# Stored low halves of projection weights, another start, and a multiply with paired operands, in a decoder-block kernel

## The chip, the cores and the metric

The kernel runs on one core of a Trainium2 chip. The metric is the device time of one execution in microseconds (us).

## The reference

One decoder block on 1024 tokens of width 1024, in float32. The conditioning vector gives six modulation vectors; two sub-layers follow, each with a norm, a shift and scale, and a gated residual.

```python
mod = silu(c) @ w_ada + b_ada
sh1, sc1, g1, sh2, sc2, g2 = split(mod, 6)
h = rms_norm(x, norm1_g) * (1 + sc1) + sh1
b_gate, c_gate, hc, q, k, v = split(h @ w_in, splits)
mixed = [norm(short_conv(b_gate, c_gate, hc)), norm(window_attention(q, k, v, rel_bias, sinks))]
x = x + g1 * (mixed @ w_out)
h2 = rms_norm(x, norm2_g) * (1 + sc2) + sh2
x = x + g2 * peer_ffn(h2, wq, keys, u_tab, v_tab)
```

`peer_ffn` scores each token against two sets of 128 keys for each of 8 heads, adds the best 16 of each set in pairs, keeps the best 16 sums, and uses those experts out of 16384 (one row of `u_tab`, one of `v_tab` each). The attention has a window of 128 and a bias per head that depends on the distance only, through 32 buckets.

## The kernel before

The tokens go through `front()` in three groups of 384, 384 and 256. A group takes 18 projections by `w_in` (keys, queries, values, and three per chunk of the convolution), the attention, 8 projections by `w_out`, and 16 by `wq`, each of the last followed by scores and a search for the 16 best. After the third group `dense()` multiplies 640 tokens with the whole expert tables and gathers single rows for the other 384.

**A projection** (`proj`, lines 260 to 274) is 42 times a group the same step: two half tiles of 128x512 (256 KB) are loaded by SP (L265). ACT casts each to `wH`, a rounded form in which TensorE (PE) multiplies fast (L268); POOL subtracts to get the rest `wL` (L269); then per half 12 matmuls, high by high, high by low and low by high (L272). `wraw`, `wH` and `wL` have three buffers each. The three groups use the same weights, so each half tile is loaded, cast and subtracted three times, 84 subtracts a group.

**Beside the projections of groups 2 and 3** run pieces of the group before, handed out by credit at each projection (`bg`, L227): `select` (the best 16 sums, then one-hot products that pick indices) and `spread`, which builds for each token a one-hot matrix `oi`, scaled, and another `oj`, multiplies them on PE (L714), copies the product to `stage` (ACT, L715), and stores `stage` in pieces of 2 MB (L717, SP). A block of 128 tokens needs 128 `oi`, dealt to the engines by the pattern `HOT = "APVV"`: 32 on ACT (L703, L704), 32 on POOL and 64 on VectorE (called DVE; both L706), and 32 `oj` on DVE (L711). The first five of the eight blocks go through `spread`; all eight go through `select`, six of them beside groups 2 and 3. In `select`, L660 compares a 128x2048 bf16 tile with ranks and L662 multiplies it by the indices `idf`, broadcast along the innermost axis; both run twice a block.

**The start** (`ada_start`, L182): parts 1 and 0 of the modulation, eight tiles of 512 KB each, arrive in turn. Part 1 is summed on DVE (L190, L192), and part 0 by PE with 128 matmuls of one column (L194). Meanwhile the statistics of the first norm are taken, and POOL scales `x` by them (L1038). Then `bias_table` (L206) makes the attention bias: each head one matmul of 32 buckets (L217), to which DVE adds a mask (L219), one by one between the first projections.

The order of instructions on each engine comes from a list scheduler over the whole program, not from the order of the lines. SP issues its DMAs strictly in that order, and one that waits holds up all that stand behind it.

Of the kernel before, what the change touches and what calls it, by code (L numbers as in the profile page):

```python
# [10 lines left out]
F32 = mybir.dt.float32  # L11
# [10 lines left out]
P = 128  # L22
# [52 lines left out]
def hymba_peer_kernel(ctx: ExitStack, tc: tile.TileContext, a, out: bass.AP):  # L75
# [39 lines left out]
    biasd = dram.tile([P, NH, 384], F32, name="biasd")  # L115

# [65 lines left out]
    def ada_start(ap, ring, acc):  # L182

        mps0 = pm.tile([P, 8], F32, name="pm")
        for c in range(NC):
            w1, w0 = ring[2 * c % len(ring)], ring[(2 * c + 1) % len(ring)]
            nc.sync.dma_start(w1, a["w_ada"][1, :, c, :])
            nc.sync.dma_start(w0, a["w_ada"][0, :, c, :])
            if c == 0:
                V.tensor_scalar(acc, w1, cond[:, c:c + 1], None, op0=ALU.mult)  # L190
            else:
                V.scalar_tensor_tensor(acc, w1, cond[:, c:c + 1], acc, op0=ALU.mult, op1=ALU.add)  # L192
# [3 lines left out]
            yield  # L196
        mps = pm.tile([P, 8], F32, name="pm")
        for m in range(NC):
            PE.matmul(mps[:, m:m + 1], acc[:, P * m:P * (m + 1)], ones[:, 0:1], start=True, stop=True)
        b0 = COLS["b"][0]  # L200
        V.tensor_add(mod[:, 8:16], mps, cols[:, b0 + 8:b0 + 16])
        V.scalar_tensor_tensor(gs[:, 0:8], mod[:, 8:16], 1.0, colr("g1"), op0=ALU.add, op1=ALU.mult)
        V.tensor_add(mod[:, 0:8], mps0, cols[:, b0:b0 + 8])
        done.extend((1, 0))

    def bias_table(ap):  # L206
        relb = ap.tile([32, NH], F32, name="relb", bufs=1)
        nc.sync.dma_start(relb, a["rel_bias"])
        bkt = ap.tile([32, 384], F32, name="bkt", bufs=1)
        nc.sync.dma_start(bkt, a["bucket"])  # L210
        bmask = ap.tile([P, 384], F32, name="bmask", bufs=1)
        nc.sync.dma_start(bmask, a["bmask"])
        rb = ap.tile([32, NH, P], F32, name="rb", tag="acc", bufs=1)
        V.tensor_copy(rb, relb.unsqueeze(2).to_broadcast([32, NH, P]))
        for h in range(NH):
            bp = pm.tile([P, 384], F32, name="pm")
            PE.matmul(bp, rb[:, h, :], bkt, start=True, stop=True)  # L217
            bt = ap.tile([P, 384], F32, name="bt", bufs=1)
            V.tensor_add(bt, bp, bmask)  # L219
            nc.sync.dma_start(biasd[:, h, :], bt)  # L220
            yield
# [3 lines left out]
    tasks, rest, table = [], [], []  # L225
# [61 lines left out]
    def norm_mod(chunk, gsc, shc, H, L, T, scaled=False, r=None):  # L287
        if not scaled and r is None:
            r = norm_stats(chunk, T)
        for c in range(NC):  # L290
# [41 lines left out]
    def front(t0, T, hs, nxt):  # L332
# [9 lines left out]
        A.copy(kc, proj(a["w_in"][4], hH, hL, T))  # L342
        qT = [tmp("y", bufs=4)[:, 0:T] for c in range(4)]
        for c in range(4):
            A.copy(qT[c], proj(a["w_in"][c], hH, hL, T))
        vT = tmp("q")
        A.copy(vT[:, 0:T], proj(a["w_in"][5], hH, hL, T))

        def conv():
            ys = []  # L350
            for cc in range(4):
                cs = tmp("q")[:, 0:T]
                A.copy(cs, proj(a["w_in"][6 + 3 * cc], hH, hL, T))
# [3 lines left out]
                V.tensor_tensor(u[:, 2:T + 2], cs, proj(a["w_in"][7 + 3 * cc], hH, hL, T), op=ALU.mult)  # L357
# [6 lines left out]
                V.tensor_tensor(y, y, proj(a["w_in"][8 + 3 * cc], hH, hL, T), op=ALU.mult)  # L364
# [34 lines left out]
        drain(table[0])  # L399
# [90 lines left out]
        for c in range(NC):  # L490
            pt = proj(a["w_out"][c], mH, mL, T)
# [101 lines left out]
    def select(va, iu):  # L593
        idf = sel.tile([P, 2 * PH, 16], BF16, name="idf")
        A.copy(idf, iu)
        va4 = va.rearrange("p (h s) k -> p h s k", s=2)
        id4 = idf.rearrange("p (h s) k -> p h s k", s=2)
        cand = sel.tile([P, PH, NCAND], F32, name="cand")
# [58 lines left out]
        for s, src in ((0, aab), (1, stb)):  # L657
# [4 lines left out]
            V.tensor_tensor(hot1, hot1, id4[:, :, s, :].unsqueeze(3).to_broadcast([P, PH, 16, 16]), op=ALU.mult)  # L662
# [357 lines left out]
    with tc.tile_pool(name="ada", bufs=2, side="right") as ap:  # L1020
# [5 lines left out]
        first = ada_start(ap, slots[0:3] + wide, slots[3])  # L1026
# [7 lines left out]
        for _ in range(3):  # L1034
            next(first)
# [94 lines left out]
```

## Time and profile before

| | |
|---|---|
| median of 3 runs | 2853.47 us (2850.66 to 2859.0) |
| profiled execution, its own time | 2857.49 us |
| span of the profiled execution | 2855.7 us |
| granted TensorE clock, mean | 0.979 |
| PE matmul busy | 2700.5 us, 95% |
| DVE busy | 2373.4 us, 83% |
| ACT busy | 1093.9 us, 38% |
| POOL busy | 1721.7 us, 60% |
| DMA moved | 764.31 MB, 268 GB/s over the span |

The first 1022 us are the three groups, the rest is the dense part. Shares over the whole span are mostly those of the dense part, so for a change in the groups each stage has to be read by itself: group 1 ends at 335 us, the `w_in` projections of group 2 at 530, its `w_out` and `wq` projections at 724, those of group 3 at 876 and 1022. A busy PE is not a PE at its peak: matmuls are pipelined, and each is shown until its modelled end.

### The profile page before, as it was taken

The page shows a single profiled execution, that of the slowest core. Times are in us where ns is not written, and L with a number is a line of the kernel's source. Part 1 is how long each engine was busy: PE and PEld are TensorE (multiplying, and loading weights), DVE is VectorE, ACT ScalarE, POOL GpSimd, SP SyncE. Part 2 cuts the span into 40 slices and gives each one's busy share as a digit, 9 for nine tenths or more (in the row PEclk, how much of TensorE's full clock was granted, in tenths as well). Part 3 has the DMA queues.
Part 4 walks back from the last instruction along what each step waited for, and adds up shares of the span by engine and source line. Part 5 has one row for each costly group of instructions (what it writes and reads, how often), then busy time and mean ns, then how long its engine had stood idle before and what let it go on. Part 6 is the DMA issues. An engine that isn't in the chain of part 4 may idle for free.

```text
span 2855.7 us, 45148 instructions
## 1 busy us (share of the span) xinstructions
PE 2700.5 (95%) x15679; PEld 2445.9 (86%) x15679; DVE 2373.4 (83%) x4845; ACT 1093.9 (38%) x2193; POOL 1721.7 (60%) x1491
## 2 busy tenths in 40 slices
PE   8899988999787889999999999999999999999998
PEld 6788978789786778889989989999989889988987
DVE  3665898877899697888988888888889888888887
ACT  2455468775586643222322222232222222222221
POOL 3444475656667744666666666666666666666661
PEclk7999999999999989999999999999999999999999
DMA  7647423464344677999999999999999999999995
GB/s 243 217 155 232 121 103 115 158 216 156 97 151 137 234 227 229 342 337 343 326 322 346 340 344 335 349 325 332 347 334 324 325 339 346 333 336 345 324 327 193
DMA packets 345157, 764.31 MB, mean 268 GB/s; under 512 B 31296, under 2 KB 130016, under 8 KB 341984
## 3 DMA queue, kind: packets, MB, share of 16 engines
q0 software_dynamic: 112320, 408.99, 39.6%
q1 hardware_dynamic: 231168, 349.81, 37.4%
q8 instruction: 123, 2.02, 0.3%
q10 hardware_dynamic: 1440, 2.62, 0.2%
q14 instruction: 106, 0.87, 0.1%
HBM read 702.06 MB, written 59.24 MB: 267 GB/s over the span
## 4 chain that ended last, share of the span: by engine, by line
PE 44%; DMA 8%; DVE 6%; issue 5%; POOL 2%; ACT 1%; SPq 0%; DVEq 0%; POOLq 0%; ACTq 0%
PE pv L873 22%; PE pa L816 21%; DMA vraw<-in_v 4%; DMA uraw<-in_uT 2%; DVE pq L768 2%; DVE vdL L860 1%; POOL rows L741 1%; ACT vdH L859 1%; DVE rows L760 1%; DMA wraw<-in_wq 1%; DMA rows<-in_v,eidx 1%; POOL uL L800 1%; DVE dacc L892 0%; DVE gw L835 0%; PE pj L272 0%
## 5 line engine op out<-in xcount | busy, mean ns | idle before, releaser
L816 PE MATMUL pa<-h,uH 128*128 128x320 f32 x4096 | 772.9, 311 | 15.2 <-ACT uH L799 6.2
L816 PEld LDWEIGHTS pa<-h,uH 128*128 128x128 f32 x4096 | 648.8, 189 | 23.1 <-ACT uH L799 7.2
L873 PE MATMUL pv<-vdH,wdH 128*128 128x512 f32 x1275 | 500.0, 392 | 18.0 <-DVE dacc L892 16.4
L269 POOL TENSOR_TENSOR wL<-wraw,wH 128x512 fp32r<-128x512 f32 x252 | 351.5, 1402 | 272.7 <-ACT wH L268 249.4
L873 PE MATMUL pv<-vdL,wdH 128*128 128x512 f32 x1275 | 497.8, 390 | 0.1
L873 PE MATMUL pv<-vdH,wdL 128*128 128x512 f32 x1275 | 496.8, 390 | 0.0
L816 PE MATMUL pa<-h,uL 128*128 128x320 f32 x2048 | 469.2, 310 | 2.3 <-POOL uL L800 2.3
L800 POOL TENSOR_TENSOR uL<-uraw,uH 128x512 fp32r<-128x512 f32 x256 | 342.4, 1338 | 163.3 <-ACT uH L799 142.7
L741 POOL DMA_INDIRECT rows<-in_u,eidx x257 | 260.8, 1015 | 157.1 <-DVE aw L760 83.2
L741 POOL DMA_INDIRECT rows<-in_v,eidx x254 | 253.7, 999 | 164.6 <-DVE pq L768 117.1
L816 PEld LDWEIGHTS pa<-h,uL 128*128 128x128 f32 x2048 | 344.6, 189 | 3.3 <-POOL uL L800 3.3
L768 DVE SCALAR_TENSOR_TENSOR pq<-rows,aw,pq 128x1024 f32<-128x1024 f32 x253 | 324.5, 1282 | 3.3 <-DMA rows<-in_v,eidx 0.8
L892 DVE TENSOR_TENSOR dacc<-dacc,pv 128x512 f32<-128x512 f32 x310 | 211.9, 684 | 134.0 <-PE pv L873 111.4
L859 ACT CAST vdH<-vraw 128x512 fp32r<-128x512 f32 x255 | 153.5, 619 | 439.0 <-DMA vraw<-in_v 366.4
L799 ACT CAST uH<-uraw 128x512 fp32r<-128x512 f32 x256 | 158.3, 619 | 418.9 <-DMA uraw<-in_uT 340.5
L760 DVE CUSTOM_DVE_ANT_0 rows<-rows,pq 128x1024 f32<-128x1024 f32 x257 | 307.5, 1212 | 12.5 <-DMA rows<-in_u,eidx 10.9
L873 PEld LDWEIGHTS pv<-vdH,wdH 128*128 128x128 f32 x1275 | 239.6, 188 | 74.9 <-DVE dacc L892 24.7
L873 PEld LDWEIGHTS pv<-vdH,wdL 128*128 128x128 f32 x1275 | 239.8, 188 | 50.9
L873 PEld LDWEIGHTS pv<-vdL,wdH 128*128 128x128 f32 x1275 | 239.8, 188 | 47.3 <-DVE vdL L860 0.5
L706 POOL TENSOR_SCALAR oi<-iota,tr 128x128 f32<-128x128 f32 x160 | 198.5, 1243 | 96.2 <-PE gps L714 88.1
L860 DVE TENSOR_TENSOR vdL<-vraw,vdH 128x512 fp32r<-128x512 f32 x255 | 192.1, 770 | 71.7 <-ACT vdH L859 66.7
L842 ACT CAST wdH<-gw 128x640 fp32r<-128x640 f32 x128 | 93.0, 728 | 377.0 <-DVE gw L835 342.4
(257 smaller groups left out, 5085.7 us busy)
## 6 DMA issues: line engine op xcount, KB each, us to landing
uraw<-in_uT SPq DMA_DIRECT2D x256, 256.0 KB
vraw<-in_v SPq DMA_DIRECT2D x255, 256.0 KB
gd<-stage SPq DMA_DIRECT2D x20, 2048.0 KB
gt<-gd SPq DMA_DIRECT2D x160, 256.0 KB
wraw<-in_w_in SPq DMA_DIRECT2D x108, 256.0 KB
wraw<-in_wq SPq DMA_DIRECT2D x96, 256.0 KB
wt<-in_w_ada SPq DMA_DIRECT2D x40, 512.0 KB
wraw<-in_w_out SPq DMA_DIRECT2D x48, 256.0 KB
```

What stands on the lines that cost most here:

```text
L269: G.tensor_tensor(wL, w, wH.bitcast(F32), op=ALU.subtract)
L706: (G if who == "P" else V).tensor_scalar(oi, iota, tr[:, 0, t:t + 1], tr[:, 2, t:t + 1], op0=ALU.is_equal, op1=ALU.mult)
L741: G.indirect_dma_start(out=r, out_offset=None, in_=table, in_offset=bass.IndirectOffsetOnAxis(ap=eidx[:, ti, k:k + 1], axis=0))
L760: V.tensor_tensor_reduce(out=r, in0=r, in1=h2, op0=ALU.mult, op1=ALU.add, scale=1.0, scalar=0.0, accum_out=aw[:, k:k + 1])
L768: V.scalar_tensor_tensor(acc, r, aw[:, k:k + 1], acc, op0=ALU.mult, op1=ALU.add)
L799: A.copy(uH, raw)
L800: G.tensor_tensor(uL, raw, uH.bitcast(F32), op=ALU.subtract)
L816: PE.matmul(AT[j][:, s, 0:n], l[:, c, :], h2[r][4 * h + c][:, s * n:s * n + n], start=(h == 0 and c == 0 and k == 0), stop=(h == 1 and c = ...
L859: A.copy(vH, raw)
L860: V.tensor_tensor(vL, raw, vH.bitcast(F32), op=ALU.subtract)
L873: PE.matmul(pt, l[:, P * tt:P * tt + P], r, start=(m == 0), stop=(m == 3 * J - 1))
L892: V.tensor_tensor(dst, dst, pt, op=ALU.add)
```

## The change

It has three parts.

1. **Stored low parts.** `proj` takes a name and an index. In the first group it keeps POOL's subtract and stores each `wL` to DRAM (`save`, one tile later); in groups 2 and 3 it loads `wL` by SP instead of subtracting. `wL` gets four buffers.
2. **The start.** Both parts are summed on DVE, part 1 first, then part 0; 8 matmuls with ones add up each. The bias table's 8 matmuls move to the beginning: the mask is a 33rd bucket with weight one, ACT copies the results out, and SP stores all 8 behind the last tile of part 0. `x` is no longer scaled by POOL; the first norm uses the way of the others, except that every second low part is made by ACT and POOL.
3. **Pairs in `select`.** ACT writes each index twice side by side (two copies a block instead of one), so that the second operand of the multiply (L662) ends in two adjacent bf16 values instead of a broadcast.

```diff
+    def save(keep):
+        while len(unsaved) > keep:
+            key, wL = unsaved.pop(0)
+            lows[key] = dram.tile([P, 4, P], F32, name="low_{}{}{}".format(*key))
+            nc.sync.dma_start(lows[key], wL.bitcast(F32))
+
-    def proj(wsrc, sH, sL, T):
+    def proj(name, m, sH, sL, T):
+        wsrc = a[name][m]
...
-            wL = wp.tile([P, 4, P], F32R, name="wL")
+            wL = wp.tile([P, 4, P], F32R, name="wL", bufs=4)
             A.copy(wH, w)
-            G.tensor_tensor(wL, w, wH.bitcast(F32), op=ALU.subtract)
+            if (name, m, h) in lows:
+                nc.sync.dma_start(wL.bitcast(F32), lows[name, m, h])
+            else:
+                G.tensor_tensor(wL, w, wH.bitcast(F32), op=ALU.subtract)
+                save(1)
+                unsaved.append(((name, m, h), wL))
```

```diff
-    def ada_start(ap, ring, acc):
...
-            for m in range(NC):
-                PE.matmul(mps0[:, m:m + 1], w0[:, P * m:P * (m + 1)], cond[:, c:c + 1],
-                          start=(c == 0 and m == 0), stop=(c == NC - 1), skip_group_check=True)
...
+    def ada_start(ring, accs):
...
+        for i in (1, 0):
+            for c in range(NC):
+                wt = ring[n % len(ring)]
+                nc.sync.dma_start(wt, a["w_ada"][i, :, c, :])
+                if c == 0:
+                    V.tensor_scalar(accs[i], wt, cond[:, c:c + 1], None, op0=ALU.mult)
+                else:
+                    V.scalar_tensor_tensor(accs[i], wt, cond[:, c:c + 1], accs[i], op0=ALU.mult, op1=ALU.add)
...
+        def fill():
+            for h in range(NH):
+                bp = pm.tile([P, 384], F32, name="pm")
+                PE.matmul(bp, rb[:, h, :], bkt, start=True, stop=True)
+                A.copy(bts[h], bp)
...
-        for c in range(NC):
-            G.tensor_tensor(x0c(c), x0c(c), r0[:, 0:T0], op=ALU.mult)
...
+            if shared and c % 2:
+                A.activation(t, t, AF.Identity, bias=shc(c))
+                G.tensor_tensor(lo, t, h.bitcast(F32), op=ALU.subtract)
```

```diff
-        idf = sel.tile([P, 2 * PH, 16], BF16, name="idf")
-        A.copy(idf, iu)
+        idf = sel.tile([P, 2, PH * 16, 2], BF16, name="idf")
+        iu4 = iu.rearrange("p (h s) a -> p h s a", s=2)
+        for s in range(2):
+            A.copy(idf[:, s].rearrange("p (h a) y -> p h a y", h=PH),
+                   iu4[:, :, s, :].unsqueeze(3).to_broadcast([P, PH, 16, 2]))
...
-            V.tensor_tensor(hot1, hot1, id4[:, :, s, :].unsqueeze(3).to_broadcast([P, PH, 16, 16]), op=ALU.mult)
+            hk = hot1.rearrange("p h a (k y) -> p (h a) k y", y=2)
+            V.tensor_tensor(hk, hk, idf[:, s].unsqueeze(2).to_broadcast([P, PH * 16, 8, 2]), op=ALU.mult)
```

The order on three engines, before and then changed. First POOL, beside the `w_out` and `wq` projections of group 2 before (`mc` is the convolution's low part):

```order
L706 TENSOR_SCALAR oi<-iota,tr 128x128 x2
L269 TENSOR_TENSOR wL<-wraw,wH 128x512
L706 TENSOR_SCALAR oi<-iota,tr 128x128
L269 TENSOR_TENSOR wL<-wraw,wH 128x512 x2
L706 TENSOR_SCALAR oi<-iota,tr 128x128 x5
L373 TENSOR_TENSOR mc_3988<-y,mc_3987 128x384 x4
L706 TENSOR_SCALAR oi<-iota,tr 128x128 x3
L269 TENSOR_TENSOR wL<-wraw,wH 128x512 x4
```

and POOL in the change, from the attention of group 2 into group 3 (L732 is the old L706, L397 the old L373):

```order
L732 TENSOR_SCALAR oi<-iota,tr 128x128 x44
L397 TENSOR_TENSOR mc_4104<-y,mc_4103 128x384 x3
L732 TENSOR_SCALAR oi<-iota,tr 128x128
L397 TENSOR_TENSOR mc_4104<-y,mc_4103 128x384
L732 TENSOR_SCALAR oi<-iota,tr 128x128 x43
L405 TENSOR_TENSOR kL<-k,kH 128x256
```

All subtracts for `wL` are gone from POOL in groups 2 and 3; what it has left there is `oi` and a few low parts of activations.

Next SP in the `w_in` projections of group 2, around the first store of `stage`, before:

```order
L265 DMA wraw_4176<-in_w_in 128x512
L265 DMA wraw_4194<-in_w_in 128x512
L265 DMA wraw_4355<-in_w_in 128x512
L265 DMA wraw_4373<-in_w_in 128x512
L717 DMA gd_87<-stage_3405 128x4096
L265 DMA wraw_4494<-in_w_in 128x512
```

and changed:

```order
L286 DMA wraw_4292<-in_w_in 128x512
L291 DMA wL_4200<-low_w_in71_791 128x512
L286 DMA wraw_4310<-in_w_in 128x512
L291 DMA wL_4295<-low_w_in80_882 128x512
L286 DMA wraw_4471<-in_w_in 128x512
L291 DMA wL_4313<-low_w_in81_902 128x512
L286 DMA wraw_4489<-in_w_in 128x512
L743 DMA gd_87<-stage_3521 128x4096
L291 DMA wL_4474<-low_w_in90_952 128x512
L286 DMA wraw_4611<-in_w_in 128x512
```

SP issues twice as many loads, and the load of a low part stands one or two places behind the load of the next `wraw`; the store of `stage` stands between them as before.

Last DVE at the start (`wt`, `wringa` and `wringb` are tiles of `w_ada` and the sums), before:

```order
L284 RECIPROCAL rstd<-rstd 128x384
L192 SCALAR_TENSOR_TENSOR wt<-wringb_145,cond,wt 128x1024
L192 SCALAR_TENSOR_TENSOR wt<-wt,cond 128x1024
L192 SCALAR_TENSOR_TENSOR wt<-wringa_142,cond,wt 128x1024
L192 SCALAR_TENSOR_TENSOR wt<-wringb_144,cond,wt 128x1024
L201 TENSOR_TENSOR mod<-pm,cols 128x8
L202 SCALAR_TENSOR_TENSOR gs<-mod,cols 128x8
L203 TENSOR_TENSOR mod<-pm,cols 128x8
```

and changed:

```order
L222 TENSOR_SCALAR wt<-wringa_142,cond 128x1024
L224 SCALAR_TENSOR_TENSOR wt<-wringa_143,cond,wt 128x1024
L230 TENSOR_TENSOR mod<-pm,cols 128x8
L224 SCALAR_TENSOR_TENSOR wt<-wringb_144,cond,wt 128x1024
L231 SCALAR_TENSOR_TENSOR gs<-mod,cols 128x8
L320 SCALAR_TENSOR_TENSOR t<-x_140,gs,rstd 128x384
L224 SCALAR_TENSOR_TENSOR wt<-wringb_145,cond,wt 128x1024
L320 SCALAR_TENSOR_TENSOR t<-x_140,gs,rstd 128x384
L224 SCALAR_TENSOR_TENSOR wt<-wt,cond 128x1024 x2
L233 TENSOR_TENSOR mod<-pm,cols 128x8
```

The second half of `mod` now waits for eight more sums on DVE instead of PE's matmuls, and two of the first norm's products stand between them.

## Rows read from the trace of the kernel before

**Rows 1.** Busy time by stage: us, each engine's busy time (instructions), PEclk, DMA share, GB/s.

```profile
0.00:335.00 335.00, 304.71 (x1618) 270.01 (x1619) 200.19 (x564) 146.66 (x315) 148.08 (x111) 0.91 0.61 198
335.00:530.00 195.00, 172.15 (x1106) 154.59 (x1104) 184.00 (x633) 138.43 (x342) 123.41 (x95) 0.97 0.37 126
530.00:724.00 194.00, 181.72 (x1117) 166.93 (x1118) 146.89 (x509) 122.34 (x273) 118.32 (x95) 0.98 0.50 168
724.00:876.00 152.00, 123.42 (x902) 110.02 (x901) 138.01 (x502) 103.81 (x255) 104.58 (x76) 0.96 0.38 129
876.00:1022.00 146.00, 125.61 (x952) 116.60 (x951) 113.70 (x389) 89.99 (x204) 106.25 (x87) 0.98 0.56 187
```

**Rows 2.** PE's instructions in time, group 2: start us, us, engine, line, tile.

```profile
...
404.77 0.34 PE L272 MATMUL pj<-hH,wH 128*128 128x384 f32 x1
...
407.37 0.34 PE L272 MATMUL pj<-hH,wH 128*128 128x384 f32 x1
408.33 1.60 PE L714 MATMUL gps<-oj,oi 128*128 128x128 f32 x12 [0.62 <-ACT stage L715]
```

**Rows 3.** Groups of PE instructions, 335 to 530 us: xcount | busy us, mean ns.

```profile
L714 PE MATMUL gps<-oj,oi 128*128 128x128 f32 x400 | 55.9, 283 | 9.2 <-DVE oi L706 3.7 <-ACT stage L715 2.5 <-DVE oj L711 1.3
```

**Rows 4.** Groups of DVE instructions by form, 335 to 1022 us, same columns.

```profile
L706 DVE TENSOR_SCALAR oi<-iota,tr 128x128 f32<-128x128 f32 x320 | 123.5, 424 | 22.9 <-PE gps L714 21.5
L711 DVE TENSOR_TENSOR oj<-iota,tr 128x512 f32<-128x512 f32 x160 | 122.4, 783 | 4.7 <-PE gps L714 2.8 <-ACT tr L690 1.4 <-issue 0.2
...
L660 DVE TENSOR_TENSOR hot<-stb,rank 128x2048 bf16<-128x2048 bf16 x6 | 7.3, 1214 | 0.0
```

**Rows 5.** Durations of tile oi in ns, min/median/max, 335 to 1022 us.

```profile
L706 DVE TENSOR_SCALAR oi<-iota,tr x320: 240/340/1379, 378.5 to 968.8; 128x128 f32<-128x128 f32 x160
```

**Rows 6.** The same of tile oj.

```profile
L711 DVE TENSOR_TENSOR oj<-iota,tr x160: 637/683/1793, 377.3 to 967.0; 128x512 f32<-128x512 f32 x160
```

**Rows 7.** POOL in time, 384 to 391 us, columns as in rows 2.

```profile
384.37 2.78 POOL L706 TENSOR_SCALAR oi<-iota,tr 128x128 f32<-128x128 f32 x2
387.12 1.27 POOL L269 TENSOR_TENSOR wL<-wraw,wH 128x512 fp32r<-128x512 f32 x1
```

**Rows 8.** DVE in time, the same stretch.

```profile
385.20 1.28 DVE L711 TENSOR_TENSOR oj<-iota,tr 128x512 f32<-128x512 f32 x2
...
387.27 1.67 DVE L711 TENSOR_TENSOR oj<-iota,tr 128x512 f32<-128x512 f32 x1
```

**Rows 9.** Busy time of L662 by stage: us, DVE busy (instructions), PEclk, DMA.

```profile
335.00:530.00 195.00, 11.49 (x5) 0.97 0.37 126
530.00:724.00 194.00, 2.29 (x1) 0.98 0.50 168
724.00:876.00 152.00, 10.73 (x4) 0.96 0.38 129
876.00:1022.00 146.00, 5.74 (x2) 0.98 0.56 187
```

**Rows 10.** Who waited for whom, 335 to 1022 us: total us, times, longest.

```profile
PE pj L272 <- POOL wL L269: 17.2, 15, 5.5
PE pj L272 <- ACT wH L268: 7.9, 5, 4.1
```

**Rows 11.** The waits of SP's queue, the same stretch.

```profile
SPq L717 <- ACT stage L715: 59.9, 9, 19.3
SPq L717 <- ACT oi L703: 36.0, 6, 14.7
```

**Rows 12.** DVE in time at the start.

```profile
15.30 1.28 DVE L192 SCALAR_TENSOR_TENSOR wt<-wt,cond 128x1024 f32<-128x1024 f32 x1 [6.67 <-DMA wt<-in_w_ada]
```

**Rows 13.** PE in time at the start.

```profile
41.14 3.55 PE L194 MATMUL pm<-cond,wt 128*128 128x1 f32 x16
...
53.18 0.69 PE L272 MATMUL pj<-hH,wH 128*128 128x384 f32 x1
...
59.08 0.91 PE L217 MATMUL pm<-bkt,rb 32*128 32x384 f32 x2
```

More of the change, by code (lines that the diff above doesn't have):

```diff
@@ L214, in bias_table @@
[L214 to L221, printed above, removed]
+        V.memset(rb, 1.0)
+        V.tensor_copy(rb[0:32], relb.unsqueeze(2).to_broadcast([32, NH, P]))
+        bts = [tmp("q") for _ in range(4)] + [tmp("y", bufs=4) for _ in range(4)]
@@ new lines, in fill, with store, total @@
+        def fill():
[3 more added lines that the diff above has]
+                A.copy(bts[h], bp)
+        def store():
+            for h in range(NH):
+                nc.sync.dma_start(biasd[:, h, :], bts[h])
+        return fill, store
+    def ada_start(ring, accs):
+        b0 = COLS["b"][0]
+        mps = [pm.tile([P, 8], F32, name="pm") for _ in range(2)]
+        def total(i):
+            for m in range(NC):
+                PE.matmul(mps[i][:, m:m + 1], accs[i][:, P * m:P * (m + 1)], ones[:, 0:1],
+                          start=True, stop=True)
+        n = 0
+        for i in (1, 0):
[6 more added lines that the diff above has]
+                    V.scalar_tensor_tensor(accs[i], wt, cond[:, c:c + 1], accs[i], op0=ALU.mult, op1=ALU.add)
+                if c == NC - 1 and i:
+                    total(1)
+                n += 1
+                yield n
+        total(0)
+        V.tensor_add(mod[:, 8:16], mps[1], cols[:, b0 + 8:b0 + 16])
+        V.scalar_tensor_tensor(gs[:, 0:8], mod[:, 8:16], 1.0, colr("g1"), op0=ALU.add, op1=ALU.mult)
+        yield n + 1
+        V.tensor_add(mod[:, 0:8], mps[0], cols[:, b0:b0 + 8])
+        done.extend((1, 0))
@@ L352, in conv @@
                 cs = tmp("q")[:, 0:T]
-                A.copy(cs, proj(a["w_in"][6 + 3 * cc], hH, hL, T))
+                A.copy(cs, proj("w_in", 6 + 3 * cc, hH, hL, T))
                 yield
@@ L1025, in hymba_peer_kernel @@
         wide = [t.rearrange("p c t -> p (c t)")[:, 0:D] for t in bigt(ba, "wringa", F32) + bigt(bb, "wringb", F32)]
-        first = ada_start(ap, slots[0:3] + wide, slots[3])
-        next(first)
-        for h in range(2):
-            nc.sync.dma_start(x0[h][:, :, 0:T0], a["xT"][:, 4 * h:4 * h + 4, 0:T0])
+        fill, store = bias_table(ap)
+        first = ada_start(slots[0:2] + wide, slots[2:4])
         def x0c(c):
             return ch(x0, c)[:, 0:T0]
-        for _ in range(3):
-            next(first)
-        r0 = norm_stats(x0c, T0)
-        for c in range(NC):
-            G.tensor_tensor(x0c(c), x0c(c), r0[:, 0:T0], op=ALU.mult)
-        for _ in first:
-            pass
-        hs = norm1(*GROUPS[0], x0c)
-        table.append(add(bias_table(ap), 1.0))
+        for n in first:
+            if n == 3:
+                for h in range(2):
+                    nc.sync.dma_start(x0[h][:, :, 0:T0], a["xT"][:, 4 * h:4 * h + 4, 0:T0])
+                fill()
+                pt0 = pj.tile([P, TM], F32, name="pj")
+                for c in range(NC):
+                    sq = tmp("sq")
+                    A.activation(sq[:, 0:T0], x0c(c), AF.Square)
+                    PE.matmul(pt0[:, 0:T0], onesd, sq[:, 0:T0], start=(c == 0), stop=(c == NC - 1))
+                r0 = tmp("rstd", bufs=2)
+                A.activation(r0[:, 0:T0], pt0[:, 0:T0], AF.Sqrt, bias=epsc)
+            if n == 2 * NC + 1:
+                V.reciprocal(r0[:, 0:T0], r0[:, 0:T0])
+        store()
+        hs = norm1(*GROUPS[0], x0c, r0)
         rest.append(add(ada((2, 4, 3, 5), ap, slots), ADA_RATE, ADA0))
         hs, prev = front(*GROUPS[0], hs, nxts[0])
+        save(0)
         for t in rest:
```

60 lines of the change are left out of this document (17 added, 43 removed).

## The prediction, made before the changed kernel was run

> **What bounds the kernel now.** I read first the busy time by stage, because the page's shares are those of the dense part. In the `w_in` stages of groups 2 and 3 (335 to 530 and 724 to 876 us) DVE is busy for 184.00 and 138.01 us, together 93% of 347 us; in the two stages of `w_out` and `wq` PE leads with 181.72 of 194 and 125.61 of 146 us, and DVE has 77% [rows 1]. PE's figures flatter it: in order of time the projections' matmuls start 0.173 us apart (2.60 us for 15 steps) but are shown 0.34 us long, and those of `spread` start 0.12 us apart (12 in 1.60 us, the last 0.28) [rows 2]. So 36 half tiles of 12 matmuls are 75 us and 400 matmuls of `spread` [rows 3] 48 us, 123 of the 195 us; attention adds some. PE could go faster there. For `w_out` and `wq` of group 2 the same count, 48 half tiles, is 100 us, plus `spread`, scores, transposes and norms, and I see little air. So: **DVE sets the pace of the `w_in` stages, PE and DVE share the others.**
>
> Next I ask what DVE's time consists of. By form, `oi` takes 424 ns and `oj` 783 ns on average [rows 4], yet their medians are 340 and 683 ns, their least 240 and 637 [rows 5, 6]. In order of time one sees why: two `oj` beside POOL's `oi` took 0.64 us each, and the next, beside POOL's subtract `wL`, took 1.67 us [rows 7, 8]. A subtract on POOL, which reads two tensors, makes a DVE instruction of two tensors wait.
>
> **The sum.** The change takes 84 subtracts from POOL in each of groups 2 and 3, 168 at 1.27 us [rows 7].
>
> *Relief of DVE.* Mean less median: (424-340) x 320 = 26.9 us for `oi`, (783-683) x 160 = 16.0 us for `oj` [rows 4 to 6]. L662 took 30.25 us for 12, 2.8 us over its free price of 2.29 us [rows 9]. That is 45.7 us in groups with 276 of DVE's 583 us; the others have fewer instructions with two tensors, and at a third of that rate give 15 more: 60 us, an estimate. Half of it I put into the `w_in` stages, which are half of the time. There L662 adds the pairs: a multiply that runs as L660 does, on the same 128x2048 bf16, would take 1.21 instead of 2.29 us [rows 4, 9]; 9 of the 12 lie there, 9 x 1.08 = 9.7 us. Of 39.7 us I let 93% come through, DVE's busy share: **-37**. The ends are -9, if the stretches stay, and -50, if two thirds lie here and all comes through. In the `w_out` and `wq` stages the other 30 us and 3 x 1.08 us fall on a DVE that is 77% busy beside a PE that is fuller; a third, **-11**, between 0 and -33.
>
> Which POOL instructions stretch DVE decides this term, and the rows above part them by one example. The Trainium skill, "SBUF — State Buffer", section "Who interferes with whom", says that a DVE instruction with two SBUF inputs contends with any GpSimd instruction that reads SBUF. By that rule POOL's `oi` would hold up `oj` as the subtract does, which the 0.64 us in rows 8 speak against; by it the term would be about half (the first rival), by the row it is the whole.
>
> *PE's own waits.* PE waited 17.2 us for `wL` from POOL [rows 10]. The part in DVE-bound time is covered; a third: **-5**, between 0 and -17.
>
> *The start.* Now PE's matmuls for part 0 end at 41.14 + 3.55 = 44.7 us [rows 13]. Changed, DVE has 16 sums of 1.28 us [rows 12], 20.5 us, and about 4 us for the reciprocal and two products that stand among them (an estimate from sizes like these), from 15.3 us on [rows 12]: 39.8 us. Half of `mod` is then still to be added up by 8 matmuls; 16 records of such one-column matmuls (two each) take 3.55 us [rows 13], so it is ready at 43.3 us, some 1 to 2 us sooner. The first projection's matmul starts at 53.18 us, and the table's matmuls come in pieces of 0.91 us between projections, as at 59.08 us [rows 13]. Four of these go, 3.6 us and as much again as they wait for, at most; taken 4. One more for the four that stood ahead of it. Together **-7**, between +3 (if DVE is stretched by 4 us more) and -10.
>
> *Stores.* 84 stores of 256 KB, 22 MB in the 335 us of group 1, are 66 GB/s on top of 198, with the DMA engines at 0.61 [rows 1]. They wait behind POOL, which they don't hold up; but in SP's order they can delay a `wraw`. Nearest row: PE's waits for `wH`, which comes from a load, 7.9 us in two groups [rows 10]. **+2**, from 0 to 8.
>
> *Loads.* In groups 2 and 3 SP loads 168 x 256 KB more, which takes the stages from between 126 and 187 GB/s [rows 1] to between 183 and 261 (22 MB over 389 and over 298 us). By rows 2 a half tile lasts at least 2.1 us on PE and 5.4 us on average in the stage of 195 us; with four buffers a load has three of them to land in. As many `wraw` loads cost PE 7.9 us [rows 10]; the new ones have less lead: **+5**, from 0 to 16 (twice that row).
>
> *At nothing:* the second copy of the indices lies on ACT, busy 71% at most in these stages [rows 1], ahead of a multiply that comes two steps later; `cand` shares `hot1`'s buffer, and DVE itself reads the one out before it writes the other. DVE's next wait, once it is faster, is for PE to free `oi` buffers, 21.5 us today [rows 4].
>
> Sum: -37 -11 -5 -7 +2 +5 = -53. From the profiled execution's 2857.5 us that is 2804.5; the median of the runs stands 4.0 us below that execution, so **2800 us**. A measurement of this kernel can tell about 0.3% from no change, 8.6 us.
>
> **The rivals.**
>
> *Half of the relief.* POOL's `oi`, now back to back, stretch DVE in the subtract's place. Subtracts are 168 x 1.27 = 213 us [rows 7] of POOL's 453 us in these stages [rows 1], so half of the 60 us would stay: -23 -6 -5 -7 +7 = -34, 2819 us. For: the part left to POOL reads SBUF too. Against: rows 7 and 8. Chance 0.13.
>
> *All of it.* Each us of DVE and each wait counts once: 60 + 13 + 17 + 7 less 2 of cost = -95, 2758 us. For: 93% busy; against: PE's fullness between 530 and 724 us. Chance 0.12.
>
> *Pairs don't pack.* If the multiply keeps 2.29 us, 9.7 x 0.93 + 3.2 / 3 = 10 us are lost: 2810 us. For: its second operand is still a broadcast over eight; against: L660's operands have a broadcast as well. Chance 0.08.
>
> *Slower.* SP issues in order, and its stores of `stage` waited 59.9 us for the copy to `stage` and 36.0 us behind ACT's `oi`, at most 19.3 us at a time [rows 11]. Today `wraw`, `wH` and `wL` with three buffers each give about six half tiles of lead; a loaded `wL` has three that PE still holds. Wherever a store waits longer than those last, 6 us at full pace and 16 us at the average, PE stops. If all 96 us reach PE: 2857.5 - 53 + 96 - 4 = 2896 us. For: 15 waits of 6.4 us on average; against: at the stages' pace most are shorter than the cover. Chance 0.07.
>
> *No change.* `spread` is a ring of PE, ACT and DVE through few buffers; if that ring sets the pace, relief turns into waits for PE: about 2853 us. Against: those waits are only 21.5 us today. Chance 0.06.
>
> **Numbers.** The forecast has 0.54; alone it spans 2775 to 2830 us. The range, 2756 to 2838 us, reaches over the two cases of relief and, at the top, over half relief with loads at their dear end; it leaves out no change, slower, and tails. Faster by over 0.3%: 0.54 + 0.13 + 0.12 + 0.08 = 0.87; within: 0.06; slower: 0.07.
>
> **What would show it.** Right: `oi` and `oj` on DVE with means near 340 and 683 ns, L662's successor at 1.2 us, the `w_in` stages of groups 2 and 3 shorter by about 37 us together and the others by 10, the first projection ending some 7 us sooner, group 1 otherwise as long as now. Wrong: means of `oj` still near 730 ns beside POOL's `oi`; PE waiting for loads of `wL` by more than 16 us; SP's waits at stores followed by gaps on PE; or a DVE that is idle for PE in the time it gained.

## The result, and the profile after

The changed kernel takes **2822.22 us** (median of 4 runs, 2820.88 to 2823.97) against 2856.23 us (4 runs) before: a ratio of 0.9883, 95% interval 0.9862 to 0.9903, 34 us faster. The forecast was 2800 us. The profiled execution has a span of 2820.3 us, 35.4 less than before.

Where the 35.4 us came from shows a table that is worked out from the starts and ends of the projections' matmuls in the two traces, in us: `start` is the first of them; `in1` the `w_in` stage of group 1 and `rest1` what follows up to the end of the group; `in23` the `w_in` stages of groups 2 and 3, `rest23` all else of these groups; `dense` from the last projection to the end.

```
             start    in1  rest1   in23 rest23   dense    span
before        53.2  140.0  142.3  342.5  344.0  1833.6  2855.7
after         54.0  137.7  150.2  294.5  340.2  1843.6  2820.3
```

The `w_in` stages give 48.0 us and `rest23` 3.8; the start costs 0.8, group 1 after it 5.6 and the dense part 10.0. Busy time by stage of the changed kernel, with columns as in [rows 1]:

```profile
0.00:342.00 342.00, 286.41 (x1510) 247.22 (x1511) 206.52 (x569) 151.96 (x328) 132.57 (x101) 0.93 0.77 259
342.00:512.00 170.00, 163.01 (x1097) 149.71 (x1096) 155.25 (x627) 136.90 (x342) 75.79 (x57) 0.99 0.56 193
512.00:707.00 195.00, 182.42 (x1128) 169.43 (x1127) 136.02 (x513) 122.05 (x276) 59.66 (x48) 0.96 0.69 239
707.00:832.00 125.00, 112.77 (x886) 104.69 (x885) 114.84 (x476) 101.17 (x252) 46.48 (x40) 0.99 0.68 234
832.00:977.00 145.00, 129.12 (x969) 122.45 (x967) 100.61 (x412) 92.98 (x212) 45.93 (x40) 0.94 0.77 269
```

In the four stages of groups 2 and 3 DVE is busy for 506.7 us where it was 582.6: 76 us less. Taken from the first to the last projection matmul of the two `w_in` stages, DVE's busy time fell from 317.6 to 269.6 us, by as much as these stages got shorter. Taken in the same way beside `w_out` and `wq`, it fell from 237.1 to 212.8 us, yet these stages did not get shorter (314.7 us before, 315.7 now); the 3.8 us of `rest23` lie in the pieces between the stages. The granted TensorE clock fell there: 0.96 and 0.94 above, 0.98 twice in [rows 1]. It stood at 1.2 GHz, the lower of its two levels, for 28.8 us of these stages, before for 6.8 us. The longest stretch, 618 to 632 us, began while PE waited for ACT's copy to `stage`:

```profile
620.47 2.93 PE L740 MATMUL gps<-oj,oi 128*128 128x128 f32 x12 [5.04 <-ACT stage L741]
...
618.00:632.00 14.00, 9.86 (x41) 9.30 (x42) 11.77 (x55) 6.91 (x16) 3.29 (x4) 0.51 0.65 225
```

22 us more at half the clock cost at most 11 us, an estimate. DMA carries 193 to 269 GB/s there instead of 126 to 187 and is nowhere full on average. The groups of DVE's instructions by form, 342 to 977 us (xcount | busy us, mean ns | idle before):

```profile
L737 DVE TENSOR_TENSOR oj<-iota,tr 128x512 f32<-128x512 f32 x160 | 107.6, 688 | 5.5 <-PE gps L740 3.6 <-ACT tr L716 0.3
L732 DVE TENSOR_SCALAR oi<-iota,tr 128x128 f32<-128x128 f32 x320 | 104.0, 361 | 39.4 <-PE gps L740 37.2 <-ACT h2H L321 0.4 <-ACT tr L716 0.2
...
L688 DVE TENSOR_TENSOR hot<-hot,idf 128x2048 bf16<-128x2048 bf16 x12 | 14.6, 1218 | 0.1
```

`oj` went from 783 to 688 ns and `oi` from 424 to 361 [rows 4], almost to their medians of before, and the multiply (L662, now L688) from 2.5 us to 1.22 us [rows 9]. The waits of PE, DVE and POOL in the same stretch:

```profile
POOL oi L732 <- PE gps L740: 161.5, 71, 10.4
...
DVE oi L732 <- PE gps L740: 37.2, 39, 7.1
...
PE pj L298 <- DMA wL<-low_wq: 3.4, 2, 2.7
```

POOL and DVE now wait longer for PE to free buffers for `oi` (DVE 37.2 us, 21.5 before [rows 4]). The increase lies beside `w_out` and `wq`: in the `w_in` stages DVE's waits of this kind, for `oi` and `oj` together, are 9.0 us and were 10.2. PE waits 3.4 us for loaded `wL` of `wq` and 1.4 us for those of `w_in`, where it waited 17.2 us for POOL [rows 10]. And SP's queue:

```profile
SPq L291 <- PE pj L298: 192.9, 110, 11.7
...
SPq L743 <- ACT stage L741: 17.8, 12, 6.6
...
SPq L743 <- ACT oi L729: 13.0, 3, 10.5
```

Its waits at the stores of `stage` for ACT's copy and `oi` fell from 95.9 us [rows 11] to 30.8; what it waits for most now is PE, which frees the buffers of `wL`.

At the start DVE and PE read as follows, in order of time:

```profile
18.41 1.28 DVE L224 SCALAR_TENSOR_TENSOR wt<-wringa,cond,wt 128x1024 f32<-128x1024 f32 x1 [4.13 <-DMA wringa<-in_w_ada]
...
26.56 2.55 DVE L1071 RECIPROCAL rstd<-rstd 128x384 f32<-128x384 f32 x1 [4.22 <-ACT rstd L1069]
...
35.74 0.17 DVE L230 TENSOR_TENSOR mod<-pm,cols 128x8 f32<-128x8 f32 x1 [2.47 <-PE pm L213]
...
48.39 0.17 DVE L233 TENSOR_TENSOR mod<-pm,cols 128x8 f32<-128x8 f32 x1 [3.67 <-PE pm L213]
...
54.00 0.69 PE L298 MATMUL pj<-hH,wH 128*128 128x384 f32 x1 [5.65 <-ACT wH L289]
```

DVE stood idle for 4.13 us at a tile, 4.22 us ahead of the reciprocal, which waited for the statistics (their matmuls stood behind the bias table's eight on PE), 2.47 us ahead of the first add to `mod`, and had the second at 48.39 us instead of 44.7 [rows 13].

### The profile page after: what moved, and what is told of

It is laid out like the page before. It is cut to its first block, busy times and chain, and to the rows that moved or that the text cites. A ratio compares the mean times of both kernels' runs of the same rounds, so it can differ in the third digit from the quotient of the medians.

```text
span 2820.3 us, 45052 instructions
## 1 busy us (share of the span) xinstructions
PE 2672.6 (95%) x15567; PEld 2428.3 (86%) x15567; DVE 2301.1 (82%) x4846; ACT 1097.0 (39%) x2213; POOL 1477.2 (52%) x1315
## 4 chain that ended last, share of the span: by engine, by line
PE 52%; DVE 7%; DMA 7%; issue 4%; ACT 2%; POOL 1%; SPq 0%; DVEq 0%; POOLq 0%; ACTq 0%
PE pv L899 25%; PE pa L842 22%; DMA vraw<-in_v 4%; PE pj L298 2%; PE gps L740 1%; DVE vdL L886 1%; DVE rows L786 1%; DVE pq L794 1%; DMA uraw<-in_uT 1%; DMA wraw<-in_wq 1%; POOL uL L826 1%; DVE dacc L918 1%; DVE gw L861 1%; DVE more L786 1%; DVE wdL L869 0%
## 5 line engine op out<-in xcount | busy, mean ns | idle before, releaser
L732 POOL TENSOR_SCALAR oi<-iota,tr 128x128 f32<-128x128 f32 x160 | 203.1, 1273 | 350.4 <-PE gps L740 161.5
L289 ACT CAST wH<-wraw 128x512 fp32r<-128x512 f32 x252 | 154.6, 618 | 165.9 <-PE pj L298 77.3
```

The lines of the kernel that those rows point to most:

```text
L732: (G if who == "P" else V).tensor_scalar(oi, iota, tr[:, 0, t:t + 1], tr[:, 2, t:t + 1], op0=ALU.is_equal, op1=ALU.mult)
```

## The experiments

Here is the same table for all of them; each has a part of its own below. The profiled execution of `k_cand` was the slowest of its 11 runs.

```
             start    in1  rest1   in23 rest23   dense    span
a_lows        53.5  142.7  152.0  295.5  336.1  1844.1  2824.0
b_start       54.6  136.7  142.1  342.8  345.3  1833.2  2854.9
c_pairs       53.6  139.6  143.0  327.4  343.8  1837.8  2845.4
d_oneinput    53.2  125.6  141.8  309.4  329.8  1830.3  2790.2
k_cand        54.0  141.1  143.2  336.8  360.2  1843.1  2878.3
f_start       40.8  132.2  152.8  296.3  338.2  1837.3  2797.7
h_winonly     54.6  137.7  143.0  295.5  346.8  1841.0  2818.9
m_candown     53.9  134.8  150.6  300.4  361.1  1830.7  2831.4
p_hot         39.7  137.4  153.1  323.6  353.3  1826.9  2834.1
n_best        40.4  135.9  148.7  296.6  343.7  1832.9  2798.2
q_dve1        40.9  133.5  153.3  295.3  335.2  1832.6  2790.6
r_nopairs     40.7  135.1  150.8  299.7  334.3  1841.0  2801.7
```

For the `w_in` stages of groups 2 and 3 a second table has DVE's busy time in them, what they last beyond it, and the granted TensorE clock in them, all worked out from the traces:

```
             in23     DVE  beyond  clock
before      342.5   317.6    24.9   0.97
after       294.5   269.6    24.9   0.99
a_lows      295.5   269.0    26.5   0.99
b_start     342.8   318.2    24.6   0.97
c_pairs     327.4   305.4    22.0   0.97
d_oneinput  309.4   285.3    24.1   0.96
k_cand      336.8   309.4    27.4   0.93
f_start     296.3   269.6    26.7   0.98
h_winonly   295.5   270.4    25.1   0.99
m_candown   300.4   270.6    29.8   0.98
p_hot       323.6   259.1    64.5   0.97
n_best      296.6   271.3    25.3   0.98
q_dve1      295.3   271.4    23.9   0.99
r_nopairs   299.7   277.8    21.9   0.99
```

In all of them but `p_hot`, the only one with another pattern of `oi`, these stages last 22 to 30 us longer than DVE is busy, whatever the clock. DVE sets their pace before the change and after it; `c_pairs`, where POOL keeps its subtracts, fits in as well.

### One part of the change at a time

`a_lows` has the stored low parts alone, `b_start` the start alone, `c_pairs` the pairs alone. `a_lows` and `c_pairs` both contain an edit that the change needs for its space:

```diff
-        cand = sel.tile([P, PH, NCAND], F32, name="cand")
+        cand = sel.tile([P, PH, NCAND], F32, name="cand", tag="hot1")
```

> The kernel before with the stored low parts alone (the old start, the old multiply; cand shares a buffer with hot1 so that the fourth wL buffer fits). If most of the gain is DVE freed from waiting beside POOL's subtracts: the w_in stages of groups 2 and 3 together about 38 us shorter than before, oj on DVE at a mean near 690 ns instead of 783, group 1 about 5 us longer (the stores), and 2822 to 2830 us in all. If the gain came from the pairs or the start instead: under 10 us.

> The kernel before with the new start alone. As forecast, the first projection starts sooner and the bias table's matmuls leave the projections: 7 us faster. Rival, read from the changed kernel's trace (DVE idle 4.2 us ahead of the reciprocal and 2.5 us ahead of the first add to mod, the first matmul at 54.0 us against 53.2): no gain at all, between 3 us faster and 1 us slower.

> The kernel before with the paired multiply alone. If DVE sets the pace of the w_in stages, 9 multiplies there save 1.08 us each: 7 to 10 us faster, with all of it in these stages, and L664 at 1.21 us where POOL does not disturb it. If a wait takes its place: under 3 us.

The ratios to before are 0.9859 (0.9841 to 0.9877), 0.9983 (0.9969 to 0.9997) and 0.9965 (0.9948 to 0.9981): 40, 5 and 10 us. Together that would be 55 us, and the change has 34. The low parts alone already shorten the `w_in` stages by 47.0 us, all but 1.0 of what the change reaches; the pairs alone give 15.1 us there. That the pairs seem to add nothing on top comes from the work that falls into these stages. The change has 9 of the 12 multiplies and 257 `oj` and `oi` of DVE in them; `a_lows` has 8 and 250, and 25 other DVE instructions fewer. It does this work beside `w_out` and `wq`, where DVE has room: it is busy there for 229.7 us, in the change for 212.8, and these stages last 314.0 and 315.7 us. So DVE has as much to do in the `w_in` stages of both, and over the groups the pairs bring nothing that can be seen. In `c_pairs` the nine multiplies take 11.3 us where they took 22.2, most of the 12.2 us by which DVE is busy for less; part of its 15.1 us belongs to the edit of `cand` (`k_cand` below has 5.7 us less in `in23`). The start brings its 3 us in `in1`, where the bias table's matmuls are gone, and not ahead of the first projection.

### What makes DVE wait beside POOL

```diff
-            G.tensor_tensor(wL, w, wH.bitcast(F32), op=ALU.subtract)
+            G.tensor_copy(wL, wH.bitcast(F32))
```

> The kernel before, but POOL makes wL by a copy of wH (one tensor read) instead of the subtract (two tensors read); the low part of the weights is so left out of the result. POOL's place, order and dependences stay, and no DMA is added. If it is the second tensor read that makes DVE wait: oj's mean near 690 ns, the w_in stages of groups 2 and 3 about 35 us shorter, 2812 to 2830 us. If it is any POOL instruction, or POOL's time and the waits for wL: oj's mean stays above 740 ns and the time within 12 us of before.

The ratio is 0.9751 (0.9733 to 0.9769), 2786.26 us. By form, and POOL's copy by line, 336 to 1000 us:

```profile
L711 DVE TENSOR_TENSOR oj<-iota,tr 128x512 f32<-128x512 f32 x160 | 113.4, 726 | 5.2 <-PE gps L714 3.7 <-ACT tr L690 1.1
L706 DVE TENSOR_SCALAR oi<-iota,tr 128x128 f32<-128x128 f32 x320 | 109.9, 382 | 22.4 <-PE gps L714 21.1
...
L269 POOL CAST wL<-wH 128x512 fp32r<-128x512 f32 x160 | 116.9, 737 | 173.0 <-ACT wH L268 168.1 <-PE pj L272 3.2 <-DVE st L651 1.5
```

and POOL's subtract in the kernel before, 335 to 1022 us:

```profile
L269 POOL TENSOR_TENSOR wL<-wraw,wH 128x512 fp32r<-128x512 f32 x167 | 233.4, 1405 | 129.5 <-ACT wH L268 123.1 <-DVE gsum L620 1.8 <-PE pj L272 1.8
```

The copy lasts 0.74 us on average where the subtract lasts 1.40 us, so POOL's time on `wL` halves, and DVE's stretch halves with it: mean less median is now (726-682) x 160 = 7.0 us for `oj` and (382-342) x 320 = 12.8 us for `oi`, 19.8 us against 42.9 before. Neither case of the expectation came: the mean of `oj` lies between the two, and the time fell further than in either. The traces also tell what POOL did beside each `oj` and `oi` of DVE; mean ns, and how many (those beside other work of POOL are left out):

```
                 oj: before   d_oneinput   oi: before   d_oneinput
POOL idle           670 (4)      672 (4)     338 (55)     336 (57)
only oi on POOL   686 (119)    688 (120)    353 (210)    357 (209)
wL on POOL        1101 (31)     803 (28)     819 (46)     520 (43)
```

A copy with a single tensor read stretches DVE too, so what I had given as the reason, that the subtract reads two tensors, does not hold as it stood. The copy does it less: against the means beside POOL's `oi`, the subtracts cost DVE 34 us in 233 us of POOL's time, the copies 10 us in 117. POOL's `oi`, 1.24 us each before, stretch next to nothing. Copy and subtract write 512 values per partition, `oi` 128; whether that is the difference was not tried. That the time falls by 71 us without any transfer shows what the contention and POOL's time are worth over all three groups: 14 us of it in `in1`, where no `spread` runs, 33 in `in23`, 14 in `rest23`. It does not part the two, since both fell; in `in23` DVE is busy for 32.3 us less. Beside `w_out` and `wq` DVE is busy for 11.4 us less and the stages are 13.6 us shorter, so less work on POOL and DVE is worth something there too; the granted clock there stayed at 0.99.

### The dense part and cand's buffer

Every kernel above with `cand` in the buffer of `hot1` is longer in its dense part. `k_cand` is the kernel before with that edit alone; `m_candown` is the change without it, with `bufs=4` taken from `wL` to make room.

> The kernel before with one edit: cand shares a buffer with hot1. The three kernels with that edit so far spent 1837.8 to 1844.1 us after the last projection, those without it 1830.3 to 1833.6. If the shared buffer does this (it holds back the next block's cand on DVE, which then takes gathered rows earlier, and POOL fetches the next rows while the dense part's first loads fill the DMA engines): that stretch 4 to 10 us longer, row fetches between 19 and 31 us after the last projection, and the kernel 0.1 to 0.4% slower. If it is the stored low parts or the faster multiply instead: no change in the stretch, which stays near 1833 us.

> The changed kernel with a buffer of its own for cand, and wL back to three buffers to make room. If the shared buffer costs the dense part 4 to 10 us: the stretch after the last projection falls from 1843.6 to 1833 to 1838 us. If three wL buffers are too few to hide the loads: the stages of groups 2 and 3 get longer, by more than 10 us, with PE waiting for wL; if the lead does not matter, they stay within 3 us.

`k_cand`: 1.0037 (1.0023 to 1.0050), and 9.5 us more in the dense part. Its profile, of its slowest run, also has `rest23` 16.2 us longer and `in23` 5.7 us shorter, with one multiply and 44 other DVE instructions fewer in the `w_in` stages; the edit moves this work too. `m_candown`: 0.9926 (0.9902 to 0.9950), so slower than the change, but 12.9 us less in the dense part. In the changed kernel POOL, PE and ACT read at the dense part's start (the last projection ended at 976.6 us):

```profile
994.78 0.96 POOL L767 DMA_INDIRECT rows<-in_u,eidx  x1 [3.61 <-DVE aw L786]
996.04 0.95 POOL L767 DMA_INDIRECT rows<-in_u,eidx  x1 [0.30 <-issue]
1003.26 0.94 POOL L767 DMA_INDIRECT more<-in_u,eidx  x1 [6.27 <-DVE pick L694]
...
1005.23 1.72 PE L842 MATMUL pa<-h,uH 128*128 128x320 f32 x5 [5.12 <-DMA h<-h2s]
...
1012.97 0.62 ACT L825 CAST uH<-uraw 128x512 fp32r<-128x512 f32 x1 [16.46 <-DMA uraw<-in_uT]
```

and in `n_best` below, with `cand` apart (last projection at 965.3 us):

```profile
983.41 0.96 POOL L773 DMA_INDIRECT rows<-in_u,eidx  x1 [4.23 <-DVE gsum L650]
...
998.72 0.96 POOL L773 DMA_INDIRECT rows<-in_u,eidx  x1 [1.60 <-DVE aw L792]
...
990.45 1.35 PE L848 MATMUL pa<-h,uH 128*128 128x320 f32 x5 [2.50 <-DMA h<-h2s]
...
995.12 0.62 ACT L831 CAST uH<-uraw 128x512 fp32r<-128x512 f32 x1 [1.91 <-DMA uraw<-in_uT]
```

With the shared buffer the next block's `cand` cannot be written while `hot1` is in use; DVE takes gathered rows in the meantime, and POOL fetches the next rows 18 to 27 us after the last projection instead of 18 and 33. ACT then waits 16.46 us for `uraw` instead of 1.91, and PE 5.12 us for `h` instead of 2.50. In the first 60 us after the last projection ACT's waits for `uraw` come to 25 to 29 us in the six kernels with the shared buffer and to 9 to 16 us in the eight without. PE's longest wait for `h` parts them less well: 3.6 to 7.2 us with it, 2.1 to 5.4 without. The 480th of the dense part's matmuls into `pa` starts 130 to 135 us after the last projection in the six kernels with the shared buffer, and 125 to 127 us in seven of the eight without. The eighth, `r_nopairs`, has 131, though it fetches rows at 19 and 42 us and its waits for `uraw` are short, 11.6 us; why, stays open. That the fetched rows take the transfers' time is argued from these rows, not tried.

The clock goes the same way. In the dense part it stood at 1.2 GHz for 45 us in the change and for 24 us before, for 35 to 46 us in the six kernels with the shared buffer and 42 in `r_nopairs`, and for 24 to 33 us in the other seven. In the change it fell to that level 27 us after the last projection, for 7 us, while PE waited its 5.12 us for `h`. 20 us more at half the clock cost at most 10 us, an estimate, and the dense part grew by 10.0. So the later loads and the clock both go with the loss; what each is worth, no run tells.

In `m_candown`, with three buffers of `wL`, `in23` and `rest23` grow by 5.9 and 20.9 us.

```profile
PE pj L298 <- DMA wL<-low_wq: 6.7, 4, 3.9
...
PE pj L298 <- DMA wL<-low_w_in: 5.8, 5, 2.9
```

PE's waits for loads come to 12.5 us (the two rows) where the change has 3.4 us for `wq` and 1.4 for `w_in`. Four buffers hide most loads of 256 KB here, three fewer of them. The waits are not all of the 27 us: beside `w_out` and `wq` PE also waited 14.3 us for ACT's copy to `stage`, in the change 7.6.

### The start put in order

```diff
+                if i == 0 and c in (LATE1, NC - 2):
+                    V.tensor_scalar(zeros[c > LATE1], accs[0][:, 0:1], 0.0, (EPS if c > LATE1 else 0.0), op0=ALU.mult, op1=ALU.add)
...
-        V.tensor_add(mod[:, 8:16], mps[1], cols[:, b0 + 8:b0 + 16])
+        V.scalar_tensor_tensor(mod[:, 8:16], mps[1], zeros[0], cols[:, b0 + 8:b0 + 16], op0=ALU.add, op1=ALU.add)
...
-                A.activation(r0[:, 0:T0], pt0[:, 0:T0], AF.Sqrt, bias=epsc)
+                A.activation(r0[:, 0:T0], pt0[:, 0:T0], AF.Sqrt, bias=zeros[1])
```

> The changed kernel, but on DVE the reciprocal stands behind the seventh sum of part 0 and the first add to mod behind the fifth (a zero made from the sum enters each, so that they can't come sooner). If the start lost its gain to DVE waiting in order, 4.2 us ahead of the reciprocal and 2.5 us ahead of the add: the first projection starts 6 to 9 us sooner than at 54.0 us, and the kernel is as much faster, 2813 to 2817 us. If the loads of w_ada set the pace: it starts at 51 us or later.

```profile
18.07 1.28 DVE L227 SCALAR_TENSOR_TENSOR wt<-wringa,cond,wt 128x1024 f32<-128x1024 f32 x1 [4.49 <-DMA wringa<-in_w_ada]
...
36.19 2.55 DVE L1077 RECIPROCAL rstd<-rstd 128x384 f32<-128x384 f32 x1 [0.67 <-ACT rstd L1076]
...
39.38 0.22 DVE L239 SCALAR_TENSOR_TENSOR mod<-pm,zero,cols 128x8 f32<-128x8 f32 x1
...
35.58 3.57 PE L216 MATMUL pm<-ones,wt 128*128 128x1 f32 x16 [8.22 <-DVE wt L227]
40.81 0.69 PE L304 MATMUL pj<-hH,wH 128*128 128x384 f32 x1 [1.66 <-ACT wH L295]
```

The first projection starts at 40.8 us, 13.2 us sooner than in the change, where 6 to 9 were expected; the ratio to before is 0.9813 (0.9779 to 0.9847), 2805 us. More came back than the two waits of 6.7 us. The reciprocal's own 2.55 us now stands beside the last eight matmuls, from 35.58 us on, so that the second half of `mod` is there at 39.38 instead of 48.39 us; and ACT's order fell out otherwise, with the first `wH` cast behind one activation of the norm instead of six. The wait at a tile behind the loads of `x`, 4.49 us, is left.

### Where the stored parts are worth it

```diff
-                unsaved.append(((name, m, h), wL))
+                if name == "w_in":
+                    unsaved.append(((name, m, h), wL))
```

> The changed kernel, but only the w_in projections store and load low parts; for w_out and wq POOL subtracts in all groups. The changed kernel gained 48 us in the w_in stages of groups 2 and 3 but 4 us in the rest of these groups, and group 1 lost 8 us in its w_out and wq stages. If the stores cost group 1 that: about 7 us come back there, w_in stays, and the w_out and wq stages of groups 2 and 3 change by at most 6 us in all: 2813 to 2822 us. If relief of DVE counts there too: they get longer by more than 10 us, and the kernel is slower than the changed one.

`rest1` falls from 150.2 to 143.0 us, as before the change, `rest23` rises from 340.2 to 346.8, `in23` stays. In all 2820.69 us, 0.9867 (0.9841 to 0.9893), not told apart from the change. So 48 of the 84 stores cost group 1 about 7 us, and what they relieve in groups 2 and 3 is worth about as much. What the stores cost it shows who waits for loads there; in the `w_out` and `wq` stages of group 1 before,

```profile
ACT wH L268 <- DMA wraw<-in_w_out: 7.5, 5, 3.4
...
ACT wH L268 <- DMA wraw<-in_wq: 2.6, 4, 1.4
```

and after:

```profile
ACT wH L289 <- DMA wraw<-in_wq: 19.1, 12, 2.8
...
ACT wH L289 <- DMA wraw<-in_w_out: 11.9, 8, 3.1
```

ACT's waits for `wraw` went from 10.1 to 31.0 us.

### What sets the pace now

`p_hot` and `r_nopairs` start from `n_best`, the next part.

```diff
-HOT = "APVV"
+HOT = "APVP"
```

> The same, but POOL makes two of four oi instead of one (pattern APVP), since POOL is idle half the time there; DVE has 160 oi of 0.36 us less, 58 us over groups 2 and 3. If DVE's work still sets the pace of the w_in stages (it is busy 91 and 92% of them in the changed kernel): they get shorter by 20 us or more together. If spread's ring of oi buffers sets it, POOL's oi of 1.27 us is the slower member: they stay as they are or get longer.

2836.09 us, 0.9919 (0.9905 to 0.9934): `in23` 27 us longer than in `n_best`, though DVE has 160 `oi` less.

```profile
DVE oi L738 <- PE gps L746: 54.2, 50, 7.1
...
DVE oj L743 <- PE gps L746: 42.1, 63, 1.3
...
PE gps L746 <- POOL oi L738: 22.3, 47, 2.1
```

DVE waits 96 us for PE to free buffers of `oi` and `oj`, and PE for POOL's `oi`. With this pattern `spread`'s ring sets the pace: the `w_in` stages last 64.5 us longer than DVE is busy. It does not follow that it sets it with the pattern of the change. There they last 24.9 us longer than DVE is busy, as before the change, and DVE's waits for PE in them did not grow.

> The kernel with the reordered start and cand apart (2795.7 us), with the old multiply and one copy of the indices again. The w_in stages with stored low parts took the same time with the old multiply (170.4 and 125.1 us) as with the new (169.8 and 124.7 us). If the pairs bring nothing once DVE no longer waits beside POOL, because spread's ring then sets the pace: within 4 us of 2795.7 us, the multiply at 2.28 us again. If DVE still sets it: 9 or 10 us slower.

```profile
L691 DVE TENSOR_TENSOR hot<-hot,idf 128x2048 bf16<-128x2048 bf16 x12 | 27.4, 2286 | 0.0
```

2802.48 us, 0.9812 (0.9794 to 0.9830), 6.8 us above `n_best` and between the two cases. The nine multiplies in the `w_in` stages take 20.5 us instead of 10.9, DVE is busy there for 6.5 us longer, and the stages are 3.1 us longer. In the profiles `dense` is 8.1 us longer, at the lower clock told above, and `rest23` 9.4 us shorter, for which I have found no cause. So this run doesn't decide what the pairs are worth over the groups.

### Two versions that beat both

`n_best` is the reordered start with `cand` in a buffer of its own; `bits` in one buffer instead of two makes the room. `q_dve1` also has the subtracts for `w_in` in group 1 on DVE:

```diff
-                G.tensor_tensor(wL, w, wH.bitcast(F32), op=ALU.subtract)
+                (V if name == "w_in" else G).tensor_tensor(wL, w, wH.bitcast(F32), op=ALU.subtract)
```

> The kernel with the reordered start, and cand in a buffer of its own again; bits in one buffer instead of two pays for it, so wL keeps four. If the shared buffer cost the dense part about 10 us and the three wL buffers the rest of the run before: the stretch after the last projection 1830 to 1835 us, the stages of groups 2 and 3 within 4 us of the changed kernel's, 2790 to 2799 us, the fastest so far. If one bits buffer is a new wait: groups 2 and 3 longer by over 5 us.

> The kernel with the reordered start and cand apart, but in group 1 the subtracts for w_in's low parts run on DVE instead of POOL, 36 of them at 0.77 us (what the same subtract takes in the dense part). The one-input run shortened that stage by 14 us, so either DVE's waits beside POOL's subtracts set it or POOL's 1.29 us did. Either way it gets shorter, by 5 to 12 us, unless 28 us more on DVE hold up the attention's chain of exp and sums there: then it is as long as now or longer.

`n_best`: 2795.69 us, 0.9778 (0.9764 to 0.9793), 26 us below the change, with `dense` at 1832.9 us. `q_dve1`: 2792.40 us, 0.9771 (0.9755 to 0.9786). `in1` shrank by 2.4 us only and `rest1` grew by 4.6, so the two are not told apart, and what the one-input run gained in `in1` is not to be had this way.

## Why the prediction was right, and where it was off

The direction, the mechanism in the `w_in` stages and the range held; the gain was 34 us where the sum gave 53. By term, the `w_in` stages gave 11 us more than the sum had for them, and the other terms missed by 29 us the other way. That the time stayed in the range is in part luck, since the two made up for each other. Point by point:

- **Relief of DVE.** I estimated 60 us of waits and 13 of the multiply; DVE's busy time fell by 76. (A third of the rate is 17 us by its own numbers, not 15, 1 us in this term.) In the `w_in` stages it fell by 48.0, and they gave 48.0 where I took 37: the multiplies are 11 of it (22.2 to 11.0 us), the rest is 37 where I put half of 60, some of that being twenty instructions that moved out of the stages, and all of it came through, not 93%. PE's waits for POOL's `wL` in these stages, 14.2 us before, went too; since DVE's share accounts for the whole, they were covered, but no run takes away the one without the other.
- **The reason for the relief** was off: `d_oneinput` shows that a copy on POOL with one tensor read stretches DVE as well. The rule of the Trainium skill, "SBUF — State Buffer", section "Who interferes with whom", is that a DVE instruction with two SBUF inputs contends with a GpSimd instruction that reads SBUF. The trace agrees for the copy, beside which `oj` takes 803 ns, and not for POOL's `oi`, beside which it takes 687 ns in the changed kernel and 683 with POOL idle, as rows 7 and 8 had it. So the rival of half the relief, though its 2819 us lie near the result, did not happen.
- **The `w_out` and `wq` stages, PE's waits for `wL`, the loads.** -11, -5 and +5; together 3.8 us came, none of it within the stages. DVE's busy time fell there by 24.3 us, and its idle time grew by 25.3. The loads cost PE 4.8 us of waits, as priced. What the sum left out is that PE's waits for the copy to `stage` grew from 1.4 to 7.6 us there and that the granted clock fell from 0.99 to 0.95, worth at most 11 us; the rest stays open.
- **The start.** -7 was forecast; the first projection starts 0.8 us later, `in1` is 2.3 us shorter. The step that failed is that DVE has 20.5 us of sums and 4 us beside them "from 15.3 us on": I added work and left out that DVE takes its instructions in order. It waited at three of them, and `f_start` took 13.2 us back by moving two.
- **The stores.** +2, with 8 as the dear end. `rest1` grew by 7.9 us, near that end: they hold up the loads of `wraw`, as the nearest row said, but more.
- **At nothing: `cand`.** This was the largest miss: 10 us in the dense part. I looked at the two tiles within one block, where DVE is in order anyway, and not at the next block's `cand`, which now waits for this block's `hot1`. How that reaches PE is argued above; the clock, for which the sum had no term, has a part in it.
- **The slower rival** did not come: SP's waits at the stores of `stage` fell by two thirds. Nor did the ring of `spread`, which I had as a cause for no change, end the gain in the `w_in` stages. Beside `w_out` and `wq` DVE's waits for it grew from 13.5 to 31.8 us.

## What to carry to other kernels

An instruction moved off a shared engine can be worth more as an end to a wait on its neighbour than by its own time; read that from the mean against the median of one form. Hold a stage's length against the busy time of its busiest engine in every run: where the difference stays the same, that engine sets the pace. Before gains in a stage are compared or added, count the work that falls into it in each run, and look at the granted clock. In a start of a few dozen us follow each engine's order row by row, and a tile that shares a buffer has to be followed into the next round of its loop, not only through its own.

## What was not expected of the hardware

Beside a copy of 128x512 on POOL (0.74 us on average) `oj` on DVE took 803 ns and `oi` 520, beside a subtract of the same size (1.40 us) 1101 and 819. Beside POOL's `oi` of 128x128, no shorter than the copy (1.24 us), they took 686 and 353, near their 670 and 338 with POOL idle. In the `w_out` and `wq` stages DVE had 24.3 us less to do and nothing got shorter, while the granted clock fell from 0.99 to 0.95.
